# A hybrid attention block on one core: the turns of q and k spread over three units, the row sums sent through DRAM

## The chip, the cores and the metric

The kernel runs on one core of one Trainium2 chip. The metric is the device time of one execution in microseconds (us); lower is better. A core has five engines that run side by side, each through its own instruction list in order: TensorE (PE, with its weight loads shown as PEld), VectorE (DVE), ScalarE (ACT), GpSimd (POOL) and SyncE (SP). All DMAs of this kernel are issued by SP, and an instruction that waits holds back everything behind it on its engine.

## What is computed

One layer of a streaming encoder over 4096 tokens of width 1024, all in float32:

```python
h = rms_norm(x, norm_g) * (1 + scale) + shift          # scale, shift, gate from c @ w_ada + b_ada
q, k, v, u, z = split(h @ w_in)                        # 512, 512, 512, 512, 1024
q = rms_norm(q per head) * q_norm_g; k = rms_norm(k per head) * k_norm_g
# 8 heads of 64; each chunk of 64 tokens sees itself and 8 chunks to the left
s = einsum('bqhd,bkhd->bhqk', qn, kn) * scale + bias   # clipped relative position
p = softmax(s); a = einsum('bhqk,bkhd->bqhd', p, vn)
# pool: trailing means over 2, 4, 8, 16 tokens minus the token, a linear map per group
y = concat(a, pool) * silu(z)
out = x + gate * (y @ w_out)
```

## The kernel before

The work has three parts. Part A (to about 575 us of the span) computes `h`, the pool branch and the gates `silu(z)`, and leaves `h` transposed (`hT_d`), the attention's gates (`gz_d`) and the pool's half of `y` (`yT_d`) in DRAM. Part B (575 to about 1730 us) is the attention. Part C multiplies `y` with `w_out`; its first twelve blocks are already mixed into the last units of part B.

Products that must keep float32 accuracy are made of a rounded part and a rest: `split` (lines 95 to 97) writes the rounded copy with ACT and the rest with POOL or DVE, and TensorE multiplies hi with hi, hi with lo and lo with hi.

Part B runs over 64 units `(ph, sg, h)`: two passes of four heads, eight groups of 512 tokens, four heads. Turn u of the loop (line 717) merges three lists of work for TensorE: the second step of unit u (`s2_items`: turn the probabilities p with TensorE, L623, split them by ACT and DVE, L629 and L630, and multiply with v, L641 and L642), the first step of unit u + 1 (`s1_items`: the products of q and k, L583 and L584, bias and row minimum by DVE, L588, exp by ACT with the row sum, L601), and one block of 128 tokens of the projection (`proj_items`: q, k, v of a block, L495 to L497). A projection block needs two halves of `h`, each loaded by `load_h` (L105) into one of two raw buffers `bhr`, then split by ACT (L96) and POOL (L97).

Before a group's q and k can be used they are turned. `tq(which, pair)` (lines 533 to 559) turns four blocks of q or k of one head pair with four TensorE transposes (L537) into a PSUM tile and writes them out for both heads: for q, ACT writes the scaled q twice, into both halves of the tile `qs` (L545, L546), and DVE the rest `ql` (L548); for k, ACT writes the scaled k (L556) and DVE its rest (L557) into `ring`. All four turns of a group stand in one unit, 4g - 2 for group g (line 713, and line 723 for the last group of a pass). `qs` has two buffers, `ring` holds three groups.

The row sums of exp come out one number per token and partition, but are needed per token along the free axis, on the partitions of the head. DVE takes the reciprocal `rl` (L606), POOL copies it 64 times side by side into `rlx` (L607), and in the unit of the odd head of a pair, half way through its products with v, `scales` turns `rlx` with four TensorE transposes (L652) and DVE multiplies the turned sums with the gate tile `gzb` (L657). `fin` adds the two halves of the product with v (L664, L665), and for the odd head POOL multiplies with `gzb` (L667) and `store_y` writes to DRAM (L334).

The order on each engine is made by the language's scheduler, which places instructions by its own model of time; the lists above give it the sequence and the dependences.

Of the kernel before, what the change touches and what calls it, by code (L numbers as in the profile page):

```python
# [10 lines left out]
F32 = mybir.dt.float32  # L11
# [39 lines left out]
def block_kernel(ctx, tc, x, xT, par, crow, w_adaT, w_in, w_uT, bias, w_pool, w_out, rcnt, out):  # L51
# [12 lines left out]
    rs_d = [dram.tile([1, SG], F32, name=f"rs_d{i}") for i in range(NSG)]  # L64
    gate_d = dram.tile([1, D], F32, name="gate_d")
# [333 lines left out]
    op = ctx.enter_context(tc.tile_pool(name="b_qk", bufs=6))  # L399
# [45 lines left out]
    with ExitStack() as cb:  # L445
# [3 lines left out]
        qp = cb.enter_context(tc.tile_pool(name="b_q", bufs=2))  # L449
# [21 lines left out]
        ring = [kp.tile([P, 3 * SG], F32R, name=f"kr{h}") for h in range(HP)]  # L471


        qlo = [[kp.tile([P, SG], F32R, name=f"ql{h}_{i}") for i in range(2 if h == HP - 1 else 1)] for h in range(HP)]
        for h in range(HP):
            z = slice((1 - h % 2) * HD, (2 - h % 2) * HD)
            for t_ in qlo[h]:
                nc.gpsimd.memset(t_[z].bitcast(F32), 0.0)

        def slot(ph, sg):  # L480
            return (ph * NSG + sg) % 3
# [50 lines left out]
        def tq_items(ph, sg):  # L532
            def tq(which, pair):
# [6 lines left out]
                for e in range(2):  # L540
                    s0 = slice(e * HD, e * HD + HD)
                    s1 = slice((1 - e) * HD, (1 - e) * HD + HD)
                    if which == 0:
                        qs = qp.tile([P, SG], F32R, name=f"qs{pair}{e}")
                        nc.scalar.activation(qs[s0], ps[s0], AF.Copy, scale=gqn[s0])  # L545
                        nc.scalar.activation(qs[s1], ps[s0], AF.Copy, scale=gqn[s0])  # L546
                        ql = qlo[2 * pair + e][(ph * NSG + sg) % len(qlo[2 * pair + e])]
# [13 lines left out]
            return [lambda w=w, p=p: tq(w, p) for p in range(2) for w in range(2)]  # L561
# [3 lines left out]
        def s1_items(ph, sg, h):  # L565
            def one(i):
# [35 lines left out]
                if i == NB - 1:  # L602
                    if e == 0:
                        rlb[pr] = wk.tile([P, NB, 2, HD], F32, name="rlx", bufs=1)
                    rl = st.tile([P, NB], F32, name="rl")
                    nc.vector.reciprocal(rl, Ls[ph, sg, h])  # L606
                    nc.gpsimd.tensor_copy(rlb[pr][:, :, e, :], rl.unsqueeze(2).broadcast_to([P, NB, HD]))  # L607
# [4 lines left out]
        def s2_items(ph, sg, h):  # L612
# [33 lines left out]
            def scales():  # L646

                gl = hold["g"] = wk.tile([P, SG], F32, name="gzb", bufs=2)
                nc.sync.dma_start(gl, gz_d[sg][ph * 2 + pr])
                ps = ptp.tile([P, SG], F32, name="ptps")  # L650
                for i in range(NB):
                    nc.tensor.transpose(  # L652
                        out=ps[:, i * P : (i + 1) * P],
                        in_=rlb[pr][:, i].rearrange("p e d -> p (e d)"),
                        identity=ident,
                    )
                nc.vector.tensor_tensor(gl, ps, gl, op=ALU.mult)  # L657
# [14 lines left out]
            for m in range(n):  # L672
                if m + LOOK < n:
                    seq.append(lambda m=m: tr(js[m + LOOK]))
                seq.append(lambda m=m: pv(m))
                if e == 1 and m == n // 2 - 1:
                    seq.append(scales)
# [25 lines left out]
        def block_items(kb):  # L703
# [8 lines left out]
            if kb[1] >= 4 and kb[1] % 4 == 0:  # L712
                for n, f in enumerate(tq_items(kb[0], kb[1] // 4 - 1)):
                    it.insert((2 if kb != (0, 4) else 9) + (5 if kb != (0, 4) else 3) * n, f)
            return it

        for u in range(-1, 64):
# [4 lines left out]
            if u in (26, 58):  # L722
                work = [none] * 6 + [f for t in tq_items(u // 58, NSG - 1) for f in (t, none, none)] + work
            if u == 27:
                work = [none] * 20 + work
# [13 lines left out]
            if u == 57:  # L739
                for n in range(2):  # L740
                    gate[n] = ring[n][:, SG : 2 * SG].bitcast(F32)
                    nc.sync.dma_start(gate[n], gate_d[:, n * 512 : (n + 1) * 512].broadcast_to([P, 512]))
# [70 lines left out]
```

## Time and profile before

| | |
|---|---|
| time, median of 3 runs | 1998.72 us (1996.77 to 2001.21) |
| the profiled execution: its time, its span | 1996.48 us, 1994.6 us |
| PE busy | 1930.3 us (97%) |
| PEld busy | 1657.0 us (83%) |
| DVE busy | 1143.5 us (57%) |
| ACT busy | 934.8 us (47%) |
| POOL busy | 851.5 us (43%) |
| mean granted TensorE clock | 0.998 of full speed |

The profiled execution took 2.2 us less than the median. The span runs from the first to the last instruction. Busy time is the time in which an engine has an instruction in flight; matmuls are pipelined and their ends are modelled, so two neighbours overlap in the rows, and the distance of two starts says what one costs. A wait row names the instruction that waited and the one that released it, with the total in us, the number of times and the longest.

### The profile page before, as it was taken

The numbers are of one execution on the slowest core, as the hardware profiler recorded it, in microseconds if no ns is written. First come the engines' busy times: TensorE is split into PE (matmuls) and PEld (weight loads), VectorE is DVE, ScalarE is ACT, GpSimd is POOL, SyncE is SP. The second block draws the span as 40 slices with busy tenths as digits, with TensorE's granted clock in tenths as the row PEclk, the third lists the DMA queues.
The fourth block names the chain that finished last, engine by engine and source line by source line (L and its number), as shares of the span: only waits on it lengthen the run. The fifth ranks groups of instructions, "written<-read, shape, count | busy, mean of one in ns | idle before, by whom it ended". The sixth has DMA issues, their size and how long they took to land.

```text
span 1994.6 us, 30020 instructions
## 1 busy us (share of the span) xinstructions
PE 1930.3 (97%) x10544; PEld 1657.0 (83%) x10544; DVE 1143.5 (57%) x2331; ACT 934.8 (47%) x1974; POOL 851.5 (43%) x1424
## 2 busy tenths in 40 slices
PE   6989999999999999999999999999999999999999
PEld 5778888888888888889888888898889788888887
DVE  7655654465635656666677666666666754333323
ACT  4422212221325656665678566756675864310121
POOL 7231332033045644445445656354445554422243
PEclk9999999999999999999999999999999999999999
DMA  9555344444431111111113222111111344544454
GB/s 331 192 174 159 103 135 145 141 123 141 148 101 53 59 58 33 44 54 43 54 52 97 74 60 64 33 59 38 43 54 43 101 142 139 180 136 149 146 181 164
DMA packets 167112, 211.76 MB, mean 106 GB/s; under 512 B 16432, under 2 KB 92720, under 8 KB 166960
## 3 DMA queue, kind: packets, MB, share of 16 engines
q1 hardware_dynamic: 166960, 209.84, 32.7%
q8 instruction: 83, 1.36, 0.3%
q14 instruction: 69, 0.57, 0.1%
HBM read 151.05 MB, written 58.74 MB: 105 GB/s over the span
## 4 chain that ended last, share of the span: by engine, by line
PE 85%; ACT 6%; DMA 3%; DVE 2%; POOL 2%; issue 2%; SPq 0%; ACTq 0%; POOLq 0%; DVEq 0%
PE ps L495 9%; PE ps L496 9%; PE ps L497 8%; PE ps L430 6%; PE ps L428 6%; PE ps L429 6%; PE ptps L623 5%; PE aps L297 4%; PE aps L298 4%; PE aps L296 4%; PE ps L297 4%; PE ps L298 4%; PE ps L296 4%; PE ops L641 3%; PE ops L642 3%; PE sps L583 3%
## 5 line engine op out<-in xcount | busy, mean ns | idle before, releaser
L97 POOL TENSOR_TENSOR bhl<-bhr,bhh 128x512 fp32r<-128x512 f32 x212 | 275.0, 1297 | 321.5 <-ACT bhh L96 313.5
L495 PE MATMUL ps<-w,bhh 128*128 128x512 f32 (+1 forms) x1024 | 353.6, 345 | 4.8 <-ACT qkr L508 4.6
L496 PE MATMUL ps<-w,bhh 128*128 128x512 f32 (+1 forms) x1024 | 352.5, 344 | 0.0
L497 PE MATMUL ps<-w,bhl 128*128 128x512 f32 (+1 forms) x1024 | 352.4, 344 | 0.0
L630 DVE TENSOR_TENSOR ptl<-ptps,pth 128x512 fp32r<-128x512 f32 x480 | 226.3, 486 | 145.6 <-ACT pth L629 142.1
L96 ACT CAST bhh<-bhr 128x512 fp32r<-128x512 f32 x224 | 138.9, 620 | 291.5 <-PE ps L429 184.9
L629 ACT CAST pth<-ptps 128x512 fp32r<-128x512 f32 x480 | 193.1, 425 | 147.2 <-PE ptps L623 132.3
L588 DVE CUSTOM_DVE_ANT_0 p<-sps,nb 128x640 f32<-128x640 f32 (+4 forms) x256 | 199.1, 778 | 86.4 <-PE sps L584 81.0
L601 ACT ACTIVATE p<-p,mx 128x640 f32<-128x640 f32 (+4 forms) x256 | 204.5, 799 | 90.7 <-DVE mx L588 89.6
L495 PEld LDWEIGHTS ps<-w,bhh 128*128 128x128 f32 x1024 | 193.7, 189 | 26.1 <-ACT qkr L508 7.9
L623 PE MATMUL ptps<-ident,p 128*128 128x128 f32 x1200 | 208.0, 274 | 3.5 <-DVE ql L548 2.9
L496 PEld LDWEIGHTS ps<-w,bhh 128*128 128x128 f32 x1024 | 193.7, 189 | 17.8
L497 PEld LDWEIGHTS ps<-w,bhl 128*128 128x128 f32 x1024 | 193.6, 189 | 17.2
L428 PE MATMUL ps<-w,bhh 128*128 128x512 f32 x512 | 200.6, 392 | 1.0 <-ACT bhh L96 1.0
L430 PE MATMUL ps<-w,bhl 128*128 128x512 f32 x512 | 200.3, 392 | 0.6 <-POOL bhl L97 0.6
L429 PE MATMUL ps<-w,bhh 128*128 128x512 f32 x512 | 200.2, 391 | 0.0
L259 POOL TENSOR_TENSOR xt<-xt,rb 128x512 f32<-128x512 f32 x56 | 80.0, 1463 | 234.2 <-DMA rb<-rs_d 234.2
L583 PE MATMUL sps<-kr,qs 128*128 128x320 f32 (+2 forms) x480 | 156.6, 334 | 13.0 <-DVE mx L588 12.3
L623 PEld LDWEIGHTS ptps<-ident,p 128*128 128x128 f32 x1200 | 144.3, 140 | 22.4 <-DVE ql L548 4.2
L641 PE MATMUL ops<-pth,v 128*128 128x512 f32 x480 | 157.7, 329 | 5.0 <-ACT pth L629 4.8
L642 PE MATMUL ops<-ptl,v 128*128 128x512 f32 x480 | 155.6, 334 | 0.1
L297 PE MATMUL aps<-hlo,w 128*128 128x512 f32 x392 | 153.6, 392 | 1.8 <-DVE hlo L97 1.8
(131 smaller groups left out, 3933.1 us busy)
## 6 DMA issues: line engine op xcount, KB each, us to landing
bhr<-hT_d SPq DMA_DIRECT2D x128, 256.0 KB, 2.7
bhr<-yT_d SPq DMA_DIRECT2D x96, 256.0 KB, 2.8
xt<-in_x_dram SPq DMA_DIRECT2D x32, 512.0 KB, 4.9
qkr<-in_x_dram SPq DMA_DIRECT2D x64, 256.0 KB, 3.4
out_dram<-qkr SPq DMA_DIRECT2D x64, 256.0 KB, 2.1
xt<-in_xT_dram SPq DMA_DIRECT2D x28, 512.0 KB, 6.5
hT_d<-xt SPq DMA_DIRECT2D x56, 256.0 KB, 2.3
w_s<-in_w_adaT_dram SPq DMA_DIRECT2D x16, 512.0 KB, 6.7
```

Source lines behind the costliest of these rows:

```text
L97: eng.tensor_tensor(lo, raw, hi.bitcast(F32), op=ALU.subtract)
L297: nc.tensor.matmul(ps, wh[:, cs], l_, start=False, stop=False)
L428: nc.tensor.matmul(ps, a_, wh, start=k == 0, stop=False)
L429: nc.tensor.matmul(ps, a_, wl, start=False, stop=False)
L430: nc.tensor.matmul(ps, l_, wh, start=False, stop=k == KT - 1)
L495: nc.tensor.matmul(ps, a_, wh, start=k == 0, stop=False)
L496: nc.tensor.matmul(ps, a_, wl, start=False, stop=False)
L497: nc.tensor.matmul(ps, l_, wh, start=False, stop=k == KT - 1)
L583: nc.tensor.matmul(o, QS[ph, sg, h][:, qc], ks[:, k0 : k0 + n], start=True, stop=False)
L623: nc.tensor.transpose(out=ps[:, i * P : (i + 1) * P], in_=Pt[ph, sg, h, i][:, w : w + P], identity=ident)
L630: nc.vector.tensor_tensor(l_[:, r], ps[:, r], a_[:, r].bitcast(F32), op=ALU.subtract)
L641: nc.tensor.matmul(o[:, r], v, a_[:, r], start=n == 0, stop=False, skip_group_check=True)
```

## The change

The turns of a group are no longer in one unit: q and k of the first head pair are turned in unit 4g - 2, q of the second pair in 4g - 1, k of the second pair in 4g, by a table `turns`. `qs` has one buffer instead of two, the rest `ql` one per head, `ring` holds two groups instead of three, and the untransposed q and k (`qkr`) get eight buffers instead of six. The second half of `qs` is no longer written by ACT but copied from the first half by a DMA from SBUF to SBUF. The reciprocal row sums are written to DRAM by a DMA of 4-byte elements (`rl_d`) and read back, broadcast over 64 partitions, into `rlb`. `scales` stands two products before the end of the unit, has no transposes, and its product runs on POOL; `gzb` has one buffer. The gate rows of part C get tiles of their own. The matrices themselves are unchanged.

```diff
-        qp = cb.enter_context(tc.tile_pool(name="b_q", bufs=2))
+        qp = cb.enter_context(tc.tile_pool(name="b_q", bufs=1))
...
-        ring = [kp.tile([P, 3 * SG], F32R, name=f"kr{h}") for h in range(HP)]
+        ring = [kp.tile([P, 2 * SG], F32R, name=f"kr{h}") for h in range(HP)]
...
-            return (ph * NSG + sg) % 3
+            return (ph * NSG + sg) % 2
...
                         nc.scalar.activation(qs[s0], ps[s0], AF.Copy, scale=gqn[s0])
-                        nc.scalar.activation(qs[s1], ps[s0], AF.Copy, scale=gqn[s0])
-                        ql = qlo[2 * pair + e][(ph * NSG + sg) % len(qlo[2 * pair + e])]
+                        nc.sync.dma_start(qs[s1].bitcast(F32), qs[s0].bitcast(F32))
+                        ql = qlo[2 * pair + e]
...
-                        rlb[pr] = wk.tile([P, NB, 2, HD], F32, name="rlx", bufs=1)
+                        rlb[pr] = wk.tile([P, SG], F32, name="rlb", bufs=2)
                     rl = st.tile([P, NB], F32, name="rl")
                     nc.vector.reciprocal(rl, Ls[ph, sg, h])
-                    nc.gpsimd.tensor_copy(rlb[pr][:, :, e, :], rl.unsqueeze(2).broadcast_to([P, NB, HD]))
+                    nc.sync.dma_start(rl_d[h].rearrange("o (b p) -> p (o b)", p=P), rl)
+                    nc.sync.dma_start(rlb[pr][e * HD : (e + 1) * HD], rl_d[h].broadcast_to([HD, SG]))
...
-                gl = hold["g"] = wk.tile([P, SG], F32, name="gzb", bufs=2)
+                gl = hold["g"] = wk.tile([P, SG], F32, name="gzb", bufs=1)
                 nc.sync.dma_start(gl, gz_d[sg][ph * 2 + pr])
-                ps = ptp.tile([P, SG], F32, name="ptps")
-                for i in range(NB):
-                    nc.tensor.transpose(
-                        out=ps[:, i * P : (i + 1) * P],
-                        in_=rlb[pr][:, i].rearrange("p e d -> p (e d)"),
-                        identity=ident,
-                    )
-                nc.vector.tensor_tensor(gl, ps, gl, op=ALU.mult)
+                nc.gpsimd.tensor_tensor(gl, rlb[pr], gl, op=ALU.mult)
...
-                if e == 1 and m == n // 2 - 1:
+                if e == 1 and m == n - 2:
                     seq.append(scales)
...
+        turns = {u: [] for u in range(-1, 64)}
+        for g in range(1, 2 * NSG):
+            t = tq_items(g // NSG, g % NSG)
+            turns[4 * g - 2] += [t[0, 0], t[1, 0]]
+            turns[4 * g - 1] += [t[0, 1]]
+            turns[4 * g] += [t[1, 1]]
...
-            if u in (26, 58):
-                work = [none] * 6 + [f for t in tq_items(u // 58, NSG - 1) for f in (t, none, none)] + work
-            if u == 27:
-                work = [none] * 20 + work
+            if u in (26, 27):
+                work = [none] * (16 if u == 26 else 20) + work
+            for n, f in enumerate(turns[u]):
+                work.insert(min(len(work), 3 + 6 * n), f)
```

The order on two engines shows what moves. The first place is ACT at the turns of group 4 (`qs` is the turned q, `kr` the ring of k, `pth` the rounded copy of the turned probabilities, `p` the probabilities, `bhh` the rounded half of `h`). Before:

```order
L545 ACTIVATE qs_8231<-ptps,gqn 64x512
L546 ACTIVATE qs_8231<-ptps,gqn 64x512
L601 ACTIVATE p,ls<-p,mx 128x640
L96 CAST bhh<-bhr 128x512
L629 CAST pth<-ptps 128x384
L545 ACTIVATE qs_8235<-ptps,gqn 64x512
L546 ACTIVATE qs_8235<-ptps,gqn 64x512
L629 CAST pth<-ptps 128x256
L96 CAST bhh<-bhr 128x512
L556 ACTIVATE kr_4534<-ptps,pt 64x512
L601 ACTIVATE p,ls<-p,mx 128x640
L629 CAST pth<-ptps 128x384
```

The other seven of the twelve half-tile writes of this group (two L545, two L546, three L556) follow in the next 17 rows. Now the same stretch, from the first q of group 4 on:

```order
L545 ACTIVATE qs_8219<-ptps,gqn 64x512
L97 CAST bhh<-bhr 128x512
L545 ACTIVATE qs_8223<-ptps,gqn 64x512
L601 ACTIVATE p,ls<-p,mx 128x640
L630 CAST pth<-ptps 128x512 x2
L508 COPY qkr<-ps 128x512
L630 CAST pth<-ptps 128x384
L601 ACTIVATE p,ls<-p,mx 128x640
L630 CAST pth<-ptps 128x256
L630 CAST pth<-ptps 128x384
L97 CAST bhh<-bhr 128x512
L556 ACTIVATE kr_4538<-ptps,pt 64x512
```

Four of the eight writes that are left come in this unit (the fourth, an L556, four rows further on); the other four stand one and two units later. (Lines below the new ones have moved by a few numbers: L629 is now L630, L105 is L106.)

The second place is SP over about one group of part B (`bhr` the raw halves of `h`, `gzb` the gate tile, `yT_d` the store of y). Before:

```order
L334 DMA yT_d_87<-osum 128x4x128
L649 DMA gzb<-gz_d_80 128x512
L105 DMA bhr<-hT_d_74 128x512 x3
L105 DMA bhr<-hT_d_75 128x512
L334 DMA yT_d_88<-osum 128x4x128
L649 DMA gzb<-gz_d_81 128x512
L105 DMA bhr<-hT_d_75 128x512 x4
```

Now:

```order
L607 DMA rl_d_103<-rl 128x4x1
L106 DMA bhr<-hT_d_75 128x512
L608 DMA rlb<-rl_d_103 64x512
L546 DMA qs_8219<-qs_8219 64x512
L335 DMA yT_d_88<-osum 128x4x128
L546 DMA qs_8223<-qs_8223 64x512
L650 DMA gzb<-gz_d_80 128x512
L106 DMA bhr<-hT_d_75 128x512 x3
L607 DMA rl_d_104<-rl 128x4x1
L608 DMA rlb<-rl_d_104 64x512
L546 DMA qs_8462<-qs_8462 64x512
L546 DMA qs_8466<-qs_8466 64x512
```

Loads of `bhr` that followed each other now have the row sums' write (L607), its read (L608, which waits until that write has landed) and the copies of q (L546) between them.

## Rows read from the trace of the kernel before

**Rows 1.** The page: PE's line of busy times, and the chain that ended last by engine.

```profile
PE 1930.3 (97%) x10544; PEld 1657.0 (83%) x10544; DVE 1143.5 (57%) x2331; ACT 934.8 (47%) x1974; POOL 851.5 (43%) x1424
PE 85%; ACT 6%; DMA 3%; DVE 2%; POOL 2%; issue 2%; SPq 0%; ACTq 0%; POOLq 0%; DVEq 0%
```

**Rows 2.** Windows: stretch and length, busy us of PE, PEld, DVE, ACT, POOL; part B.

```profile
575.00:1640.00 1065.00, 1035.06 (x6503) 915.55 (x6501) 684.84 (x1619) 691.05 (x1545) 556.46 (x1168) 1.00 0.20 61
```

**Rows 3.** Windows: one of sixteen stretches with a group's turns, and the sixteen summed.

```profile
875.50:901.00 25.50, 24.18 (x154) 21.05 (x153) 19.20 (x42) 22.16 (x46) 7.65 (x17) 1.00 0.14 42
...
sum 400.80, PE 374.54 PEld 318.69 DVE 288.48 ACT 338.14 POOL 157.03; mean PE 23.41 PEld 19.92 DVE 18.03 ACT 21.13 POOL 9.81
```

**Rows 4.** Windows: two slices of 6 us inside one of these stretches.

```profile
882.00:888.00 6.00, 5.55 (x42) 4.95 (x40) 5.17 (x11) 5.42 (x12) 1.35 (x2) 1.00 0.28 97
888.00:894.00 6.00, 5.13 (x30) 3.93 (x30) 4.78 (x12) 5.86 (x13) 1.44 (x2) 1.00 0.00 0
```

**Rows 5.** Waits of PE, 640 to 1640 us: total us, times, longest.

```profile
PE sps L583 <- DVE mx L588: 11.9, 24, 1.0
PE ops L641 <- ACT pth L629: 4.8, 10, 0.9
```

**Rows 6.** Groups of instructions by line: busy us, mean ns of one, idle before.

```profile
L546 ACT ACTIVATE qs<-ptps,gqn 64x512 fp32r<-64x512 f32 x64 | 43.7, 683 | 0.8
L556 ACT ACTIVATE kr<-ptps,pt 64x512 fp32r<-64x512 f32 x64 | 43.7, 683 | 4.6 <-PE ptps L537 1.9 <-DVE kr L557 1.3
L545 ACT ACTIVATE qs<-ptps,gqn 64x512 fp32r<-64x512 f32 x64 | 43.6, 682 | 6.5 <-PE ptps L537 3.6 <-DVE ql L548 1.9
...
L607 POOL COPY rlx<-rl 128x256 f32<-128x256 f32 x64 | 25.4, 397 | 78.3 <-DVE rl L606 69.7 <-PE ps L429 2.9 <-DVE rqw L81 2.1
...
L652 PE MATMUL ptps<-ident,rlx 128*128 128x128 f32 x128 | 19.5, 272 | 0.0
```

**Rows 7.** Timeline of PE around one `scales`: start, us, line, tile.

```profile
866.02 0.34 PE L641 MATMUL ops<-pth,v 128*128 128x384 f32 x1
866.19 0.49 PE L623 MATMUL ptps<-ident,p 128*128 128x128 f32 x3
866.43 0.42 PE L642 MATMUL ops<-ptl,v 128*128 128x384 f32 x1
866.70 0.60 PE L652 MATMUL ptps<-ident,rlx 128*128 128x128 f32 x4
867.05 0.36 PE L496 MATMUL ps<-w,bhh 128*128 128x256 f32 x1
867.25 0.22 PE L583 MATMUL sps<-kr,qs 128*128 128x128 f32 x1
```

**Rows 8.** Groups by line: the product of q and k in three of its shapes.

```profile
L583 PE MATMUL sps<-kr,qs 128*128 128x320 f32 x288 | 93.5, 332 | 8.1 <-DVE mx L588 7.5 <-DVE kr L557 0.3
...
L583 PE MATMUL sps<-kr,qs 128*128 128x512 f32 x48 | 21.2, 442 | 1.8 <-DVE mx L588 1.8
...
L583 PE MATMUL sps<-kr,qs 128*128 128x128 f32 x48 | 11.9, 248 | 0.0
```

**Rows 9.** DMA issues: count, KB, median us to landing; then SP's wait for the first.

```profile
bhr<-hT_d SPq DMA_DIRECT2D x128, 256.0 KB, 2.7
...
rs_d<-rxy SPq DMA_DIRECT2D x7, 2.0 KB, 7.9
...
SPq L179 <- DMA rs_d<-rxy: 53.2, 7, 9.0
```

**Rows 10.** Timeline of SP in part B: start, us, line, transfers.

```profile
851.44 20.04 SPq L105 DMA_DIRECT2D bhr<-hT_d  x4
...
882.09 26.60 SPq L105 DMA_DIRECT2D bhr<-hT_d  x4
```

**Rows 11.** The same in the last units, where blocks of part C are mixed in.

```profile
1648.67 0.32 SPq L105 DMA_DIRECT2D bhr<-yT_d  x1
...
1653.90 0.32 SPq L105 DMA_DIRECT2D bhr<-yT_d  x1
```

**Rows 12.** Timelines of DVE and of POOL at the same moment.

```profile
865.19 1.17 DVE L80 TENSOR_SCALAR rqv<-ssq 128x8 f32<-128x8 f32 x1
866.39 0.17 DVE L81 TENSOR_SCALAR rqw<-rqv 128x8 int32<-128x8 int32 x1
...
865.04 1.29 POOL L97 TENSOR_TENSOR bhl<-bhr,bhh 128x512 fp32r<-128x512 f32 x1 [0.61 <-ACT bhh L96]
```

More of the change, by code (lines that the diff above doesn't have):

```diff
@@ L64, in block_kernel @@
     rs_d = [dram.tile([1, SG], F32, name=f"rs_d{i}") for i in range(NSG)]
+    rl_d = [dram.tile([1, SG], F32, name=f"rl_d{i}") for i in range(4)]
     gate_d = dram.tile([1, D], F32, name="gate_d")
@@ L396, in block_kernel @@
                 nc.sync.dma_start(gate_d.rearrange("o (j p) -> p (o j)", p=P), mod[:, 16:24])
-    op = ctx.enter_context(tc.tile_pool(name="b_qk", bufs=6))
+    op = ctx.enter_context(tc.tile_pool(name="b_qk", bufs=8))
     WO = {}
@@ L469, in block_kernel @@
         gk = pt[:, C_GK : C_GK + 1]
-        ring = [kp.tile([P, 3 * SG], F32R, name=f"kr{h}") for h in range(HP)]
-        qlo = [[kp.tile([P, SG], F32R, name=f"ql{h}_{i}") for i in range(2 if h == HP - 1 else 1)] for h in range(HP)]
+        ring = [kp.tile([P, 2 * SG], F32R, name=f"kr{h}") for h in range(HP)]
+        qlo = [kp.tile([P, SG], F32R, name=f"ql{h}") for h in range(HP)]
         for h in range(HP):
             z = slice((1 - h % 2) * HD, (2 - h % 2) * HD)
-            for t_ in qlo[h]:
-                nc.gpsimd.memset(t_[z].bitcast(F32), 0.0)
+            nc.gpsimd.memset(qlo[h][z].bitcast(F32), 0.0)
         def slot(ph, sg):
-            return (ph * NSG + sg) % 3
+            return (ph * NSG + sg) % 2
         Vt, QK, QS, QL = {}, {}, {}, {}
@@ L559, in tq @@
                         )
-            return [lambda w=w, p=p: tq(w, p) for p in range(2) for w in range(2)]
+            return {(w, p): (lambda w=w, p=p: tq(w, p)) for p in range(2) for w in range(2)}
         Pt, Ot, Ls, rlb = {}, {}, {}, {}
@@ L711, in block_items @@
             it = proj_items(*kb, after=nx)
-            if kb[1] >= 4 and kb[1] % 4 == 0:
-                for n, f in enumerate(tq_items(kb[0], kb[1] // 4 - 1)):
-                    it.insert((2 if kb != (0, 4) else 9) + (5 if kb != (0, 4) else 3) * n, f)
-            return it
+            if kb == (0, 4):
+                t = tq_items(0, 0)
+                for n, wp in enumerate(((0, 0), (1, 0), (0, 1), (1, 1))):
+                    it.insert(9 + 3 * n, t[wp])
+            return it
+        turns = {u: [] for u in range(-1, 64)}
[4 more added lines that the diff above has]
+            turns[4 * g] += [t[1, 1]]
         for u in range(-1, 64):
@@ L740, in block_kernel @@
                 for n in range(2):
-                    gate[n] = ring[n][:, SG : 2 * SG].bitcast(F32)
+                    gate[n] = bp.tile([P, 512], F32, name=f"gate{n}")
                     nc.sync.dma_start(gate[n], gate_d[:, n * 512 : (n + 1) * 512].broadcast_to([P, 512]))
```

## The prediction

> **What bounds the kernel now.** First the page's busy times and the chain that ended last [rows 1]: TensorE is busy 97% of the span and carries 85% of the chain. So what counts is what the change takes off TensorE's own list, and which of TensorE's waits it opens or closes. Time saved on ACT, DVE or POOL counts only where TensorE waits for them. An average over the span hides where TensorE is not full, so the windows come next. In part B, from 575 to 1640 us, TensorE is busy 1035.1 of 1065 us [rows 2]: 29.9 us are open. Sixteen stretches of 18 to 29 us, one around each group's turns of q and k, take 400.8 us together, and TensorE is busy in 374.5 of these [rows 3]. That is 26.3 us open in the turns and 3.6 us in all the rest of part B. In the turns ACT is the full engine: 22.2 of 25.5 us in the example [rows 3], and 5.86 of 6 us in the slice where TensorE has only 5.13 [rows 4]. The waits of TensorE say the same from the other side: it waits for DVE's row minimum, which frees the one score tile in PSUM, and for ACT's rounded copy of the probabilities [rows 5]. Both queue on their engines between the writes of the turned q and k. So part B has two prices to look at: TensorE's instructions outside the turns, and ACT's crowd inside them.
>
> The sum below is made against the profiled execution's own time of 1996.5 us. It is 2.2 us below the median of the three runs, about one part in a thousand, so I make no correction for it; 0.2% (4 us) is about what a measurement of this kernel can tell from no change.
>
> **The change part by part.**
>
> (a) *The transposes of the row sums go.* 128 transposes in 32 sets of four. A set's price is read from two starts [rows 7]: from the product L642 at 866.43 to L583 at 867.25 it is 0.82 us, in which stand the four transposes, the 384 columns of L642 and the 256 of L496. The 384 columns of L641 take 0.17 us from start to start (866.02 to 866.19), so 256 take about 0.11 to 0.12. Left for the set are 0.53 us; 32 x 0.53 = 17 us. The group's busy time, 19.5 us [rows 6], is the upper bound, since ends overlap. If a set hides its weight loads better elsewhere, a lower bound is three transposes' distance in the same rows, 0.24 us from 866.19 to 866.43, hence 0.08 each and 10 us in all. I take 17, because the set itself was measured between two starts. TensorE is full where these stand, so they are on the path: -17 us.
>
> (b) *The turns are spread, and ACT writes q once.* Before, a group has twelve half-tile writes of 0.683 us on ACT (four each of L545, L546 and L556 [rows 6]), 8.2 us inside one unit. Now the four of L546 are DMAs (64 in all, 43.7 us of ACT), and the eight left, 5.5 us, are spread: 2.7 us in the first unit, 1.4 us in each of the next two, as the order of ACT shows. In the example ACT goes from 22.2 busy us of 25.5 to about 22.2 - 8.2 + 2.7 = 16.7, or 65%, about what it has over all of part B (691 of 1065 us [rows 2]). There TensorE loses next to nothing. Bounds: at best all 26.3 us come back; at worst only the share of the writes that disappear, 4 of 12, so 9 us. I take 20, nearer the best, because the 3.6 us in the rest of part B show what TensorE loses when ACT is no fuller than this: -20 us. What is late next are the single PSUM tile of scores and DVE's row minimum behind it [rows 5].
>
> (c) *One buffer for q, two groups in the ring.* Group g overwrites group g - 2 in the ring, and the last products that read it (heads 0 and 1 of group g - 1) run two units before the first k is turned; for the second pair the same holds by one or two units. The same count holds for q. So the writes find their buffers free, and cost nothing; without that cover each would wait for at most a unit. But with a ring of two, six groups instead of five have the previous group's keys not side by side with their own. One group more is 16 row blocks (four heads of four blocks); half of them have a 512 and a 128 wide product for two of 320, the others 384 and 256. By the rows 442 + 248 = 690 ns stand against 2 x 332 = 664 [rows 8], 26 ns more, twice with the rest's product: 16 x 0.05 us is +1 us at most, below nothing only if a wide product hides a load better. I take +1 us.
>
> (d) *The row sums go over SP.* 64 writes of 4-byte elements, 64 reads. The same form stands in part A: the write lands 7.9 us after issue, and SP stands still 53.2/7 = 7.6 us for it before it can issue the read [rows 9]. If part B is like it, SP stands 64 x 7.6 = 486 us, in about 1100 us. Nobody waits for the sums themselves: they are ready at the end of one unit and used at the end of the next, some 17 us on (1100/64), against 7.6 + 4 for write and read. What is queued behind the wait matters: the loads of the raw halves. One half is used every 8.6 us (128 halves in 1100 us) and there are two raw buffers, so a load has about 17 us from the moment its buffer is free to its use. SP's rows show four loads drawn out over 20.0 and 26.6 us, each waiting for a buffer, not for data [rows 10]. The chain is 7.6 (write) + 0.3 (issue) + 2.7 (load [rows 9]) = 10.6 us, plus some 2 us for ACT's and POOL's split: covered. In the last six units it is tight: there loads follow each other every 5.2 us [rows 11], so two buffers give 10.5 us against 12.6. Twelve heads' worth of loads at most 2 us late: up to 24 us, nothing below if the lists are not that tight. I take 4 us, nearer nothing, since only loads that stand directly behind a read of the sums can be late: +4 us. The copies of q wait for ACT and have at least a turn's time before their first use; hidden. The gate tile is loaded, as before, right after the previous pair's store.
>
> The Trainium skill speaks against this form: DMA: Bandwidth & Descriptors, under its rules for kernel authors, says a strided last dimension becomes one descriptor per element and should be rearranged. Part A's 7.9 us for 2 KB agree with it [rows 9]. The same page, in its anatomy of one DMA, gives a fixed cost of about 2.0 us; by that the term in (d) would be zero and the sum 1960.5 us, but the measured row decides.
>
> (e) *POOL, DVE.* POOL loses 64 copies of 0.40 us [rows 6] and gains 32 products like its subtraction of 128 x 512, 1.29 us [rows 12]: +16 us on an engine busy 52% of part B [rows 2]. DVE loses 32 products. A two-input product of POOL can hold up a small operation of DVE: L80 took 1.17 us beside POOL's L97, its neighbour L81 0.17 [rows 12]. 32 more such products hold DVE for 32 us at most, spread over 1065 us in which DVE is idle 380. I take 0 for TensorE; if that cover is gone, a held operation delays a row minimum by 1 us.
>
> **Sum:** 1996.5 - 17 - 20 + 1 + 4 = 1964.5, so **1965 us**.
>
> **The rivals.**
>
> *The turns still cost what they cost.* The idle time of TensorE in the turns could come less from ACT than from the one score tile in PSUM, whose release by DVE is the longest wait [rows 5]; spreading ACT's writes would not help it. For it: 11.9 us stand at that wait. Against it: ACT has 98% in the slice where TensorE loses most [rows 4]. Then (b) gives 4 to 9 us: 1996.5 - 17 - 6 + 1 + 4 = about 1979, up to 1985.
>
> *SP becomes the bound (slower).* Place: the read of the row sums on SP, with loads of the next halves behind it. If a load has not two but one period of lead, 8.6 us, then the chain of 10.6 us and 2 us of split is 4 us late; with a load right behind in every head TensorE stands 64 x 4 = 256 us, in every fourth head 64. With 64: 1996.5 - 36 + 64 = about 2024. It decides from 36/64 = 0.56 us per head: below that the kernel is still faster. For it: 486 us of standing still on the one queue that feeds everything. Against it: today SP's loads wait for buffers, not the buffers for loads [rows 10].
>
> *More comes back than is seen.* Matmul ends are modelled, so TensorE can be slowed in the turns while it shows busy. The slice 888 to 894 has 30 matmuls, the one before 42 [rows 4], at mixed sizes. If the turns give all 26.3 us, the sets the upper 19.5, SP costs nothing and some 4 us of hidden slowing go too: 1996.5 - 26 - 19.5 - 4 + 1 = 1948.
>
> **How the numbers follow.** The forecast, 1957 to 1973, has 0.64; the turns still cost 0.18; more comes back 0.11; SP bounds 0.07. The range reaches from the third rival to above the first: 1946 to 1988; outside it lie SP as the bound and some of the edges. Faster by over 0.2%: the forecast, more, and nearly all of the first rival, 0.91; within 0.2%: 0.03; slower: 0.06.
>
> **What would show it.** Right: no L652, PE's busy time down by 15 to 20 us, the windows around the turns with TensorE open for under 10 us in all sixteen, ACT there near 65 to 75%. Wrong in (b): TensorE still open by 20 us there, at the row minimum. Wrong in (d): ACT's cast of `bhh` waiting for its load in part B, where no such wait is listed now, and TensorE waiting for `bhh` or `bhl`. Right in (d): the write of the sums lands in 5 to 8 us, and SP waits for it some 300 to 500 us in all while TensorE doesn't notice.

## The result: 8% slower

The changed kernel took 2158.76 us (median of 4 runs, 2152.99 to 2163.01) beside 1999.53 us for the kernel before on the same chip: a ratio of 1.0796 with a 95% interval of 1.0767 to 1.0825. I had said 1965 us, and 1946 to 1988 for the range. In what follows 0.0010 of a ratio is about 2.0 us.

The page of the changed kernel, PE's busy times and the chain by engine, against [rows 1]:

```profile
PE 1969.7 (92%) x10416; PEld 1680.4 (78%) x10416; DVE 1110.8 (52%) x2299; ACT 890.6 (41%) x1910; POOL 865.2 (40%) x1391
PE 20%; DMA 5%; issue 2%; POOL 1%; DVE 1%; ACT 0%; SPq 0%; POOLq 0%; ACTq 0%; DVEq 0%
```

TensorE has 128 instructions fewer and is busy 39 us longer. The second line can't be set against the one in [rows 1]: its shares add to 29%, because the chain as it is followed here reaches back only to about 1528 of 2151 us. In that last stretch 2.7% of the span, some 58 us, are landings of the row sums' write.

The windows say where (in part A's 575 us PE is busy 546.57 us, as before; here is part B, against [rows 2], and the last units):

```profile
575.00:1640.00 1065.00, 961.96 (x5810) 844.08 (x5810) 586.41 (x1436) 574.04 (x1320) 511.21 (x1063) 0.96 0.26 64
1640.00:1760.00 120.00, 89.10 (x476) 76.12 (x475) 53.38 (x121) 59.42 (x130) 55.14 (x70) 0.86 0.35 102
```

In the same 1065 us TensorE issues 5810 matmuls instead of 6503, is open for 103 us instead of 30, and its granted clock is 0.96 instead of 1.00. PE, DVE, ACT and POOL all do less in the stretch; none has become the full one. The waits, SP's, POOL's, ACT's and PE's (engine and line, what it waited for, us, times, longest):

```profile
SPq L608 <- DMA rl_d<-rl: 497.1, 63, 10.1
SPq L106 <- POOL bhl L98: 190.5, 93, 8.5
...
POOL gzb L651 <- DMA rlb<-rl_d: 277.4, 26, 21.0
...
ACT bhh L97 <- DMA bhr<-hT_d: 41.6, 14, 7.5
...
PE sps L583 <- DVE mx L588: 33.2, 24, 8.0
PE ps L497 <- POOL bhl L98: 26.8, 7, 5.7
PE ops L642 <- ACT pth L630: 26.5, 12, 8.7
```

And the DMA issues (count, KB each, median us from issue to landing), against [rows 9]:

```profile
bhr<-hT_d SPq DMA_DIRECT2D x128, 256.0 KB, 3.2
...
qs<-qs SPq DMA_DIRECT2D x64, 128.0 KB, 4.5
rlb<-rl_d SPq DMA_DIRECT2D x64, 128.0 KB, 4.2
...
yT_d<-osum SPq DMA_DIRECT2D x32, 256.0 KB, 4.7
...
rl_d<-rl SPq DMA_DIRECT2D x64, 2.0 KB, 8.2
```

SP stands 7.9 us for each write of the row sums; I had written 7.6. What I had written off as covered is not: ACT waits 41.6 us for loads of `h` in part B, where before it was 1.1, and POOL waits 277 us for the row sums. One head shows how the parts hang together (merged timeline; the brackets hold the idle time and its releaser):

```profile
882.47 0.18 DVE L606 RECIPROCAL rl<-ls 128x4 f32<-128x4 f32 x1 [0.99 <-ACT p L601]
882.68 0.37 SPq L607 DMA_DIRECT2D rl_d<-rl  x1
...
892.73 0.47 SPq L608 DMA_DIRECT2D rlb<-rl_d  x1
...
895.72 1.26 POOL L651 TENSOR_TENSOR gzb<-rlb,gzb 128x512 f32<-128x512 f32 x1 [10.19 <-DMA rlb<-rl_d]
896.94 1.26 POOL L98 TENSOR_TENSOR bhl<-bhr,bhh 128x512 fp32r<-128x512 f32 x1
...
898.25 0.76 PE L497 MATMUL ps<-w,bhl 128*128 128x512 f32 x1 [4.54 <-POOL bhl L98]
...
898.82 0.63 PE L642 MATMUL ops<-pth,v 128*128 128x512 f32 x1
...
899.24 0.63 PE L643 MATMUL ops<-ptl,v 128*128 128x512 f32 x1
```

The write is issued at 882.68 and SP can issue the read only at 892.73. POOL's order has the product with the gate right behind the read, so POOL stands 10.19 us, with the split of `h` behind it, and TensorE stands 4.54 us for that. Then its matmuls come at little more than half the pace: 512 columns of L642 start 0.42 us before the next instruction (898.82 to 899.24), where two of 512 in the projection stood 0.23 us apart a moment earlier (889.40 to 889.63); the windows give a granted clock of 0.79 and 0.78 of full speed for 896:900 and 900:904, a mixture of the levels of 2.4 and 1.2 GHz.

The DMA engines over time, 881.9 to 893.9 in 40 slices of 0.3 us (busy share in tenths, then GB/s):

```profile
DMA  0000025000000000000000070000000000000000
GB/s 0 0 0 0 0 2 5 0 0 0 0 0 0 0 0 0 0 0 0 0 0 0 0 55 0 0 0 0 0 0 0 0 0 0 0 0 0 0 0 0
```

The 512 pieces of the write are through the DMA engines within 0.6 us. From there to 892.73 they move nothing but one block of instructions, and yet SP still waits for the write to land. So, as far as these rows show, it is neither the issue nor the engines' work on the pieces that takes the 8 us.

Here nothing else is slowed, because nothing else is under way: the read is SP's next DMA and stands until the write has landed. It is so behind 42 of the 64 writes; behind the other 22 SP issues another transfer first.

### The profile page after: what moved, and what is told of

It is laid out like the page before. It is cut to its first block, busy times and chain, and to the rows that moved or that the text cites. A ratio compares the mean times of both kernels' runs of the same rounds, so it can differ in the third digit from the quotient of the medians.

```text
span 2151.2 us, 29973 instructions
## 1 busy us (share of the span) xinstructions
PE 1969.7 (92%) x10416; PEld 1680.4 (78%) x10416; DVE 1110.8 (52%) x2299; ACT 890.6 (41%) x1910; POOL 865.2 (40%) x1391
## 5 line engine op out<-in xcount | busy, mean ns | idle before, releaser
L497 PE MATMUL ps<-w,bhl 128*128 128x512 f32 (+1 forms) x1024 | 358.9, 350 | 26.8 <-POOL bhl L98 26.8
L495 PE MATMUL ps<-w,bhh 128*128 128x512 f32 (+1 forms) x1024 | 360.0, 352 | 11.0 <-ACT qkr L508 8.0
L496 PE MATMUL ps<-w,bhh 128*128 128x512 f32 (+1 forms) x1024 | 358.3, 350 | 0.9 <-POOL w L98 0.9
L630 ACT CAST pth<-ptps 128x512 fp32r<-128x512 f32 x480 | 193.1, 425 | 152.3 <-PE ptps L624 110.6
L624 PE MATMUL ptps<-ident,p 128*128 128x128 f32 x1200 | 221.5, 281 | 15.7 <-DVE ptl L631 7.9
L495 PEld LDWEIGHTS ps<-w,bhh 128*128 128x128 f32 x1024 | 198.3, 194 | 30.2 <-ACT qkr L508 8.5
L496 PEld LDWEIGHTS ps<-w,bhh 128*128 128x128 f32 x1024 | 198.2, 194 | 19.8 <-POOL w L98 1.2
L429 PE MATMUL ps<-w,bhh 128*128 128x512 f32 x512 | 204.1, 399 | 8.1 <-ACT bhh L97 5.2
L430 PE MATMUL ps<-w,bhh 128*128 128x512 f32 x512 | 203.4, 397 | 0.0
L642 PE MATMUL ops<-pth,v 128*128 128x512 f32 x480 | 167.5, 349 | 28.7 <-ACT pth L630 26.5
L583 PE MATMUL sps<-kr,qs 128*128 128x320 f32 (+2 forms) x480 | 161.4, 343 | 35.2 <-DVE mx L588 33.2
L624 PEld LDWEIGHTS ptps<-ident,p 128*128 128x128 f32 x1200 | 149.9, 143 | 37.6 <-DVE ptl L631 8.8
L651 POOL TENSOR_TENSOR gzb<-rlb,gzb 128x512 f32<-128x512 f32 x32 | 40.9, 1278 | 337.8 <-DMA rlb<-rl_d 277.4
L643 PE MATMUL ops<-ptl,v 128*128 128x512 f32 x480 | 160.9, 344 | 13.2 <-DVE ptl L631 12.7
```

The lines of the kernel that those rows point to most:

```text
L429: nc.tensor.matmul(ps, a_, wh, start=k == 0, stop=False)
L430: nc.tensor.matmul(ps, a_, wl, start=False, stop=False)
L495: nc.tensor.matmul(ps, a_, wh, start=k == 0, stop=False)
L496: nc.tensor.matmul(ps, a_, wl, start=False, stop=False)
L497: nc.tensor.matmul(ps, l_, wh, start=False, stop=k == KT - 1)
L624: nc.tensor.transpose(out=ps[:, i * P : (i + 1) * P], in_=Pt[ph, sg, h, i][:, w : w + P], identity=ident)
```

## The experiments

Each kernel is compared with the kernel before on the same chip, and the numbers are ratios to it.

### Which part of the change it is

There were three theories at first. A: POOL's product waits for the read, with the splits of `h` behind it. B: SP stands for the write to land, so what is queued on it comes late. C: the loss is in the spread turns, the single buffers and the ring of two.

**e1_sums_by_pe** puts the row sums of the kernel before into the changed kernel:

```diff
-                    nc.sync.dma_start(rl_d[h].rearrange("o (b p) -> p (o b)", p=P), rl)
-                    nc.sync.dma_start(rlb[pr][e * HD : (e + 1) * HD], rl_d[h].broadcast_to([HD, SG]))
+                    nc.gpsimd.tensor_copy(rlb[pr][:, :, e, :], rl.unsqueeze(2).broadcast_to([P, NB, HD]))
...
-                if e == 1 and m == n - 2:
+                if e == 1 and m == n // 2 - 1:
```

> The changed kernel with one part undone: the row sums are copied by POOL, turned by TensorE and multiplied by DVE again, in the middle of the unit. Theory A (the loss is POOL's product, which waits for the read of the row sums with the splits of h behind it): 1965 to 1990 us, the turns' gain without the transposes' gain. Theory B (the loss is SP standing still for the write, so that loads come late): the same 1965 to 1990 us. Theory C (the loss is the spread turns, the single buffer of q, the smaller ring or the copy of q by DMA): about 2150 us, as the changed kernel.

Measured: 0.9953 (0.9939 to 0.9968), 1992.48 us, a little above the interval that A and B gave.

**e2_sums_dram_only** is the reverse, the kernel before with those lines of the change alone.

> The kernel before with one part done: the row sums through DRAM, their product late and on POOL; turns, buffers and ring as before. Theories A and B: slower than before by at least 100 us, 2100 to 2180 us. Theory C: 1975 to 1990 us, the transposes' gain alone.

Measured: 1.1372 (1.133 to 1.1415), 2275.27 us, above the 2100 to 2180 that A and B gave. C falls: what costs is in the row sums, and it costs more without the spread turns.

**e3_no_wait_pool** takes POOL's wait away:

```diff
-                nc.gpsimd.tensor_tensor(gl, rlb[pr], gl, op=ALU.mult)
+                nc.gpsimd.tensor_tensor(gl, ones, gl, op=ALU.mult)
```

> The changed kernel, but POOL's product reads a tile of ones in place of the row sums that were read back; the write and the read stay on SP, so the output lacks the division by the row sums. Theory A: 1960 to 1995 us, with SP still standing some 500 us for the writes. Theory B: 2100 us or more, little different from the changed kernel. Theory C: about 2150 us.

Measured: 1.1033 (1.1012 to 1.1054), 2207.81 us. POOL's wait moved rather than went. Of this run, SP's and POOL's:

```profile
SPq L610 <- DMA rl_d<-rl: 568.3, 64, 11.2
...
POOL gzb L653 <- DMA gzb<-gz_d: 218.5, 27, 14.4
```

Now the same product waits for the gate tile, which also comes over DMA. A as I had put it, POOL's wait for the row sums, is not the root. That this run is slower than the changed kernel is not explained; SP's wait has grown from 497 to 568 us.

**e4_no_write** removes the 64 writes; the reads fetch a row of ones that is written once:

```diff
-                    nc.sync.dma_start(rl_d[h].rearrange("o (b p) -> p (o b)", p=P), rl)
```

> The changed kernel without the 64 writes of the row sums; the reads stay and fetch a row of ones that was written once, so the output lacks the division by the row sums, and SP never stands for a write. Theory A: the read no longer follows 8 to 10 us behind the write, so POOL's wait shrinks to a few us in all and the time is 1960 to 1995 us. Theory B: the same 1960 to 1995 us. Theory C: about 2150 us.

Measured: 0.9897 (0.9881 to 0.9914), 1981.05 us. So 64 writes of 2 KB, with the waits that they cause, are worth 0.0899, some 180 us.

### Is it SP's wait, or the write itself?

e4 takes away both. **f1_write_no_wait** keeps the writes and takes only the wait:

```diff
-                    nc.sync.dma_start(rlb[pr][e * HD : (e + 1) * HD], rl_d[h].broadcast_to([HD, SG]))
+                    nc.sync.dma_start(rlb[pr][e * HD : (e + 1) * HD], one_d.broadcast_to([HD, SG]))
```

> The changed kernel with all 64 writes of the row sums kept; only the reads fetch a row of ones that is written once, so that SP never has to wait for a write to land (the output lacks the division by the row sums). Theory B (SP standing still for the landing, with the loads queued behind it, is the loss): as fast as the kernel without the writes, 1975 to 1995 us, and the wait for rl_d gone from SP's list. Rival T (the 512 elements of 4 bytes of each write load the DMA engines and slow the other transfers, whoever waits): 2100 to 2170 us, with loads of the halves that land later than 3 us.

Measured: 1.0551 (1.0535 to 1.0568), 2113.67 us: theory T's number, far from B's. Nothing waits for rl_d in this run any more, but:

```profile
SPq L107 <- DMA bhr<-hT_d: 68.1, 15, 11.1
...
POOL gzb L655 <- DMA gzb<-gz_d: 117.6, 20, 12.2
```

The loads themselves now land late: the first row is SP, which waits for the load before to land, up to 11.1 us at a time and 68.1 us in all; in the kernel before it was at most 1.6 and 15.3. Taking the wait away gives back 0.0245 (1.0796 - 1.0551), 49 us; writes that nobody waits for still cost 0.0654 (1.0551 - 0.9897), 131 us. That does not make the wait worth only 49 us in the changed kernel: where SP no longer stands, it issues into the time in which the write lands, and the wait is exchanged for slow transfers.

**f2_whole_rows** lets each partition write its four sums side by side:

```diff
-                    nc.sync.dma_start(rl_d[h].rearrange("o (b p) -> p (o b)", p=P), rl)
+                    nc.sync.dma_start(rl_d[h].rearrange("o (p b) -> p (o b)", p=P), rl)
```

> The changed kernel with one edit: each partition writes its four row sums side by side, 128 pieces of 16 bytes in place of 512 of 4 bytes; SP still waits for the landing before the read (the row sums come back in another order, so the output is divided by those of other rows). Theory B: the time follows SP's wait per head; if the landing drops from 8 to about 4 us, the loss drops by more than half, 1990 to 2060 us. Rival W (any wait on SP behind a DVE result costs the same, however long): above 2100 us.

Measured: 0.9915 (0.9899 to 0.9932). The write lands in 2.1 us, and SP waits 87.6 us in all instead of 497.1. W falls. The time is below the 1990 to 2060 us that B gave; the result alone can't tell B from T.

**f3_read_by_act** lets ACT issue the read, placed half a unit later in the program.

```diff
+            def fetch():
+                nc.scalar.dma_start(rlb[pr][e * HD : (e + 1) * HD], rl_d[h].broadcast_to([HD, SG]))
...
+                if m == n // 2 - 1:
+                    seq.append(fetch)
```

> The changed kernel, computing the same; the read of the row sums is issued by ACT in the middle of the next unit, when the write should have landed, and no longer by SP. Theory B: SP's wait for rl_d goes, ACT waits for it little, 1975 to 2000 us. If the engine that issues the read has to stand for the write wherever it is put, ACT stands instead and it stays above 2080 us. Theory A's remainder (POOL's product waiting for its read) would show as 2020 to 2080 us with POOL's wait for rlb still above 200 us.

Measured: 1.2174 (1.2148 to 1.22), 2437.41 us, the slowest of all. The scheduler set the read close behind the write in ACT's order, presumably because its model of time has the write landed early, and ACT stood for it (in one head SP issued the write at 877.46, and ACT, idle for 8.40 us, could issue the read at 886.95):

```profile
ACT pth L629 <- DMA rl_d<-rl: 218.7, 24, 11.4
...
ACT qs L545 <- DMA rl_d<-rl: 91.5, 11, 11.0
```

So standing for the landing costs more on ACT, for whose copies of p TensorE waits 221.5 us in this run, than on SP (1.2174 against 1.0796). The experiment did not test what it was meant to, a read that comes after the landing; that stays untried.

It shows something else. SP, which no longer waits, goes on issuing while the write lands. Of the head above (the transfers issued between 877 and 889; count, KB, us from issue to landing):

```profile
bhr<-hT_d SPq DMA_DIRECT2D x1, 256.0 KB, 9.1
yT_d<-osum SPq DMA_DIRECT2D x1, 256.0 KB, 9.9
...
rl_d<-rl SPq DMA_DIRECT2D x1, 2.0 KB, 9.5
```

The load issued 0.5 us behind the write takes 9.1 us, the store of y 9.9, and a copy of q, from SBUF to SBUF, 8.7. Over the run, 22 loads of `h`, 8 stores of y and 14 copies of q were issued before the write ahead of them had landed, with medians of 11.1, 10.0 and 8.9 us; for those issued in the 5 us after a landing the medians are 2.8, 2.9 and 2.5. So loads, stores and copies inside SBUF are all slow while such a write lands.

**g1_idle_writes** tests the write by itself. It is e1_sums_by_pe, with the writes added and nobody reading them:

```diff
+                    nc.sync.dma_start(rl_d[h].rearrange("o (b p) -> p (o b)", p=P), rl)
                     nc.gpsimd.tensor_copy(rlb[pr][:, :, e, :], rl.unsqueeze(2).broadcast_to([P, NB, HD]))
```

> The kernel with the row sums turned by TensorE (e1_sums_by_pe, 1992 us), and beside that the 64 writes of the row sums to DRAM, which nobody reads. Nothing waits for these writes. Theory B (SP standing still for the landing is the loss): 1990 to 2010 us. Theory T (the 512 pieces of 4 bytes keep the DMA engines from the transfers behind them): 2080 to 2150 us, with TensorE's waits for bhh, bhl or the copies of the probabilities back.

Measured: 1.0381 (1.0352 to 1.0409), 2079.91 us, against 0.9953 without the writes: 0.0428, 86 us for 128 KB that nobody reads. B alone falls: the writes cost this where nobody stands for them. In the changed kernel, where SP does stand, both can be at work.

**g3_write_by_act** is f1_write_no_wait with the writes on ACT's queue:

```diff
-                    nc.sync.dma_start(rl_d[h].rearrange("o (b p) -> p (o b)", p=P), rl)
+                    nc.scalar.dma_start(rl_d[h].rearrange("o (b p) -> p (o b)", p=P), rl)
```

> As f1_write_no_wait (writes kept, reads fetch a row of ones, the output lacks the division), but the writes are issued by ACT and so go over another DMA queue than the loads. Theory Q (a write holds only what stands behind it in its own queue): 1980 to 2015 us. Theory T (the pieces keep the DMA engines busy for all queues): 2080 to 2130 us, like f1_write_no_wait's 2114. ACT may wait some tenths of a us per head for the row sums, which alone would be hidden.

Measured: 1.0493 (1.0477 to 1.0508), beside f1's 1.0551. Another queue gives back 0.006 of 0.065, so Q falls.

### What in the write it is

The slices of the DMA engines above already speak against T in the form I gave it: the engines are not busy with the pieces. Two forms were left: by N the price is the number of pieces, by L it is that the pieces land close together.

**h1_idle_apart** has the same 512 pieces as g1_idle_writes, 64 bytes apart:

```diff
-    rl_d = [dram.tile([1, SG], F32, name=f"rl_d{i}") for i in range(4)]
+    rl_d = [dram.tile([1, 16 * SG], F32, name=f"rl_d{i}") for i in range(4)]
...
-                    nc.sync.dma_start(rl_d[h].rearrange("o (b p) -> p (o b)", p=P), rl)
+                    nc.sync.dma_start(rl_d[h].rearrange("o (b p z) -> p (o b) z", p=P, z=16)[:, :, 0], rl)
```

> g1_idle_writes (1.0381 of the kernel before) with the 512 pieces of 4 bytes of each write laid 64 bytes apart; still nobody reads them. Theory N (the number of pieces is the price, wherever they land): no change, 1.03 to 1.045. Theory L (pieces that land close together in DRAM wait for each other, and the transfers behind wait with them): most of the loss goes, 0.995 to 1.015, and a row of 2 KB behind a write no longer runs at some 20 GB/s.

Measured: 0.9953 (0.9938 to 0.9968), the same as without any writes. This kernel and g1_idle_writes give TensorE and SP the same instructions in the same order and move the same 205872 packets; in g1 these keep the 16 DMA engines busy for 39.2% of a span of 2081.7 us, here for 36.3% of 1993.0. At one place in part B the writes stand between the same neighbours. Here are the DMA engines over 12 us there, in slices of 0.3 us, the write issued in the third. g1_idle_writes, pieces side by side, 941.2 to 953.2:

```profile
DMA  0000035000015961000008363995907799908722
GB/s 0 0 0 0 0 3 4 0 0 0 0 14 157 273 246 55 0 0 0 0 0 41 7 55 14 14 14 7 14 14 7 14 20 20 14 0 27 20 7 14
```

h1_idle_apart, 64 bytes apart, 927.6 to 939.6:

```profile
DMA  0000035000005795000006882000000000000000
GB/s 0 0 0 0 0 3 4 0 0 0 0 7 96 225 321 198 27 0 0 0 0 137 321 321 75 20 0 0 0 0 0 0 0 0 0 0 0 0 0 0
```

The pieces take the same two slices in both. Two loads of 256 KB are issued from 1.9 us after the write on. With the pieces apart, the first is through in six slices and the second in five, at up to 321 GB/s. With the pieces side by side, some 224 KB pass in the first five slices (the sum of the second row there, times 0.3 us); what is left of the two then crawls at 7 to 27 GB/s in most slices, the DMA engines mostly busy, for over 5 us. N falls, and it is how close the pieces lie that decides, as L had it; that they wait for each other is L's picture, and no row shows it.

**h2_idle_quarter** writes one sum per partition, 128 pieces side by side:

```diff
-                    nc.sync.dma_start(rl_d[h].rearrange("o (b p) -> p (o b)", p=P), rl)
+                    nc.sync.dma_start(rl_d[h].rearrange("o (b p) -> p (o b)", p=P)[:, 0:1], rl[:, 0:1])
```

> g1_idle_writes with a quarter of each write: one of the four row sums per partition, 128 neighbouring pieces of 4 bytes, nobody reads them. Theory N or L with a price in proportion to the pieces: a quarter of the 86 us, about 1.005. A price that needs a long row of pieces: 0.994 to 0.998, no loss. A price per write, whatever its size: 1.03 and more.

Measured: 1.0232 (1.0203 to 1.0261), between the cases I named: 0.0279 for 128 pieces, 0.0428 for 512. The price is not in proportion to the pieces: 128 of them land after 8.3 us (median), as 512 do after 8.2 in the changed kernel. And 128 of 4 bytes side by side cost 56 us, where f2's 128 of 16 bytes with SP's waits for them cost 0.0018 (f2 against e4), 4 us.

**h4_idle_16b** lays the 512 pieces 16 bytes apart (`z=4` in the place of `z=16`).

> g1_idle_writes with the 512 pieces of 4 bytes laid 16 bytes apart, so that four of them share 64 bytes of DRAM, as four partitions' pieces of 16 bytes do in g2_rows_reordered. If only pieces side by side hurt: 0.994 to 0.998, like h1_idle_apart's 0.9953. If any pieces of 4 bytes within the same 64 bytes hurt: 1.01 to 1.04.

Measured: 0.9973 (0.9963 to 0.9982). Some 0.002 is left of the 0.043, hardly clear of noise, though four pieces share 64 bytes. The slow forms have 16 pieces in each 64 bytes of DRAM (g1, h2), the fast ones four (f2, h4) or one (h1). Whether the pieces must touch to be slow, or whether it is their number within a stretch, these runs do not separate.

### The parts of the gain, and a version faster than both

**e6_spread_only** is e1_sums_by_pe with the second half of q written by ACT again:

```diff
-                        nc.sync.dma_start(qs[s1].bitcast(F32), qs[s0].bitcast(F32))
+                        nc.scalar.activation(qs[s1], ps[s0], AF.Copy, scale=gqn[s0])
```

> The kernel before with the spread turns, one buffer for q and the ring of two alone; the row sums turned by TensorE, both halves of q written by ACT. The prediction's term (b) without its DMAs: ACT keeps 12 writes of 0.68 us per group, spread over three units; 1980 to 1995 us if the spreading is what gives the gain, 1995 to 2003 us (no change) if it was the four writes taken from ACT.

Measured: 0.9981 (0.9971 to 0.999). The spreading alone gives 4 us; the four writes per group taken from ACT give another 0.0028 (to e1), 6 us. Both are small: the intervals of the two runs lie 0.0003 apart.

**h3_rows_alone** is the kernel before with the row sums alone, 16 bytes per partition.

> The kernel before with the row sums through DRAM alone, written 16 bytes per partition as in g2_rows_reordered; turns, buffers and ring as before. It gives term (a) of the prediction by itself, at a write that lands in 2 us: 0.991 to 0.996 if the transposes are worth 8 to 17 us; it was 1.1372 with pieces of 4 bytes (e2_sums_dram_only), which had the crowd of the turns beside it. Above 1.0 if the crowd of the turns, not the pieces, was what made e2 so slow.

Measured: 0.9985 (0.9975 to 0.9994), above the expected interval, where the same with 4-byte pieces had 1.1372. The crowd of the turns did not make e2 slow; but beside it the pieces cost 0.139 (1.1372 - 0.9985), and with the turns spread 0.088 (1.0796 - 0.9921, the next run).

**g2_rows_reordered** is the changed kernel with f2's write, computing the same as the kernel before:

```diff
+                nc.gpsimd.tensor_tensor(
+                    gl.rearrange("q (b p) -> q b p", p=P),
+                    rlb[pr].rearrange("q (p b) -> q b p", b=NB),
+                    gl.rearrange("q (b p) -> q b p", p=P),
+                    op=ALU.mult,
+                )
```

> The changed kernel with each partition's four row sums written side by side (16 bytes, as f2_whole_rows), and POOL's product reading the returned row in the order in which it was written, so that it computes the same as the kernel before. Both B and T: like f2_whole_rows, 1983 to 1995 us, faster than the kernel before and than the changed kernel. If POOL reads the row with its step of 16 bytes more slowly, 32 products of at most 2 us more lie beside TensorE's work.

Measured: 0.9921 (0.9906 to 0.9935), 1987.14 us: 15 us faster than the kernel before. Its writes land in 2.0 us. Read in this order, POOL's product takes 1.56 us instead of the 1.28 of the changed kernel; f2, where it takes 1.29, has 0.9915. SP's wait and part B's window:

```profile
SPq L608 <- DMA rl_d<-rl: 91.2, 61, 2.6
```

```profile
575.00:1640.00 1065.00, 1041.42 (x6453) 918.68 (x6452) 658.67 (x1591) 650.00 (x1484) 590.77 (x1143) 1.00 0.28 78
```

TensorE is busy 1923.4 us with the same 10416 instructions that took 1969.7 in the changed kernel, and part B's granted clock is 1.00 again instead of 0.96: so some 46 us of the loss lay in matmuls that ran at the lower clock level behind the gaps, as in the example above.

## Why the prediction was wrong

**(d), the row sums over SP: +4 forecast, some +180 measured (after against e4_no_write). This is the step that failed.** Its first half was right: the write lands in 8.2 us, SP stands 497 us, as part A's rows had said [rows 9]. What failed is that the wait would be hidden: the chain "7.6 (write) + 0.3 (issue) + 2.7 (load [rows 9]) = 10.6 us, ... covered", and "Nobody waits for the sums themselves". The runs show two costs in its place.

One is the wait itself. Behind 42 of the 64 writes the read is SP's next DMA, and what stands behind it starts some 8 us late. The sums are waited for: "used at the end of the next" unit is the place of the use in the program, but on POOL the scheduler had set the product right behind the read, 0.3 to 25 us (median 10.5) ahead of the instruction that needs it, and POOL stands 277 us there, with the split of `h` and TensorE behind it. And "two raw buffers" is a lead only while loads land in time.

The other is one that the prediction did not have. I priced the load behind the write with the 2.7 us of a load that has no such write near it, but what is issued while the write lands is slow: 11.1 us for a load of `h` in f3. With no wait at all (f1), on another queue (g3) or with nobody reading (g1), 64 such writes cost 131, 119 and 86 us. Part A's rows could not show this: there SP itself stands for the write, so nothing was issued in those 8 us. The prediction should have asked why 2 KB need three times as long as 256 KB, and bounded the load behind the write by the write's own 7.9 us.

How the 180 us of the changed kernel divide between the two is not shown, since each takes the other's place. What is shown is that both go when the write lands in 2 us: g2, with all its waits and reads, is only 0.0024 (5 us) above e4, about the +4 that I had.

**(a), the transposes: -17 forecast, 3 to 11 us measured.** TensorE's busy time falls by 16.7 us from e1 to e4 (1934.2 to 1917.5), as forecast, but the time by 0.0056, 11 us. The rows held that number too: in [rows 7] the four transposes themselves take 0.35 us from their start to the next (866.70 to 867.05), 11 us in 32 sets. With real writes of 16 bytes it is 0.0032 (e1 to g2), 6 us, and in the unspread kernel 0.0015 (h3), 3 us. The rest became open time: part B's window has TensorE open for 17.0 us in e1 and 23.6 in g2. I had taken it that on a full engine each instruction removed shortens the time by as much.

**(b) and (c), turns and buffers: -19 forecast, -9 measured (e1).** TensorE's open time in part B falls from 29.9 to 17.0 us, 13 of the 20 that I took; its busy time rises from 1930.3 to 1934.2, where (c) had 1. The first rival (1979 to 1985, the turns cost what they cost) had sized this better than the forecast. By these runs six tenths of the gain (0.0028 of 0.0047, neither far above its interval) came from the four writes moved to a DMA, which lands in 2.3 us in e1. So the spreading of the eight writes left, on which the step leaned, gave the smaller part.

**(e), POOL and DVE: 0.** g2 has all 32 products on POOL and is no slower than e1, which has none; no run speaks against it.

**The rivals.** "SP becomes the bound" had the right side and place with 0.07 and 2024 us; its point of 0.56 us per head was passed fivefold (180/64 = 2.8 us), in part by a mechanism that it did not name. Its evidence against, that SP's loads wait for buffers [rows 10], was true of a kernel without the writes. The sign I had given as wrong in (d), ACT's cast of `bhh` waiting for its load in part B, is what the profile shows (41.6 us).

**The Trainium skill** had the right sign: DMA: Bandwidth & Descriptors, in its rules for kernel authors, speaks against a strided last dimension because it becomes one descriptor per element. Its reason is not the one that decides here: h1_idle_apart has as many elements, and its ratio is e1's. The 2.0 us of its anatomy of one DMA, which that section gives for DMAs issued by GpSimd, is near what the writes took in g2 (2.0) and h1 (2.2), not the 8.2 of the 4-byte neighbours. The same page, in its section Issuing engines are not separate DMA queues, says that starting DMAs from several engines saves little more than the time to start them; g3_write_by_act agrees, with 0.006 of 0.065.

## What to carry to other kernels

When a small DMA takes far longer to land than its bytes explain, ask both who waits for it and what else is in flight during that time; a kernel that happens to stand still for it, as part A does, hides the second. Test a suspected write by adding it to a kernel that does not need it. For many small values, let each partition write its values side by side and let the consumer read them in that order through its access pattern: here this turned 1.0796 into 0.9921, for 0.28 us more per product on POOL.

## What was not expected of the hardware

- 512 writes of 4 bytes, side by side in DRAM, are through the DMA engines in 0.6 us and land after 8.2 us (median, changed kernel). 64 bytes apart the same 512 land in 2.2 us, 16 bytes apart in 2.9, and 128 of 16 bytes side by side in 2.1.
- While such a write lands, other transfers are slow: in f3 loads from DRAM took 11.1 us and copies inside SBUF 8.9 (medians), against 2.8 and 2.5 just after a landing. In g1 what was left of two loads behind such a write crawled at 7 to 27 GB/s in most slices for over 5 us, where their twins reached 321. Why most of the first load had passed fast before that is not explained; nor is why neighbouring 4-byte pieces are slow and neighbouring 16-byte pieces are not.
- After a gap of 4.5 us TensorE's 512-column matmuls started 0.42 us apart instead of 0.23, at granted clocks of 0.79 and 0.78 in the next two windows of 4 us.
